# A hybrid decoder trunk on one core: Newton steps, low parts and weight sums on GpSimd, copies and scalings on ScalarE

## The chip, the cores and the metric

The kernel runs on one core of a Trainium2 chip. The core has five engines that work side by side: TensorE (PE, matrix products and transposes; PEld is its weight load), VectorE (DVE), ScalarE (ACT), GpSimd (POOL) and SyncE (SP, which here only issues DMAs). Each engine takes its instructions in order from a queue of its own and waits at an instruction until the semaphores that it needs have been raised. The metric is the device time of one execution in microseconds.

## What is computed

One layer of a decoder for a prompt of 2048 tokens and 8 single sample tokens, with model width 1024, and a final RMSNorm. The reference, cut and shortened to what matters here:

```python
ada = jax.nn.silu(c) @ w_ada + b_ada
shift, scale, gate = jnp.split(ada, 3, axis=-1)
hn = _rmsnorm(x, g_norm) * (1.0 + scale[:, None]) + shift[:, None]
z = hn @ w_in
xa, za, q, k, v, glr, zg = jnp.split(z, SPLITS, axis=-1)
...
xc = conv_b + sum(xp[:, j:j + T] * conv_w[j] for j in range(CONV_W))
gx = sigmoid(blockdiag(xc, w_gate_x) + b_gate_x)
ga = sigmoid(blockdiag(xc, w_gate_a) + b_gate_a)
...
_, h = lax.associative_scan(_lin_comb, (a, u), axis=1)
y_lru = h * jax.nn.silu(za)
...
def step(S, xs):
    qn, kn, vn, dl = xs
    o = jnp.einsum('bhck,bhkv->bhcv', qn, S)
    S = jnp.exp(dl[:, :, 0, :])[..., None] * S + jnp.einsum('bhck,bhcv->bhkv', kn, vn)
    return S, o
...
o = o * lax.rsqrt(jnp.mean(o * o, axis=-1, keepdims=True) + EPS) * g_gla_norm
y_gla = o.reshape(Bn, T, D_GLA) * jax.nn.silu(zg)
mix = jnp.concatenate([y_lru, y_gla], axis=-1) @ w_out
x = x + gate[:, None] * mix
```

There are 4 heads of gated linear attention (GLA; keys 128 wide, values 256) and 8 tiles of 128 channels of the recurrent group (LRU).

## The kernel before

**Halves, heads, chunks.** The prompt is worked in two halves of 1024 tokens. The first has two segments of 512 tokens, the second three of 384, 384 and 264, the last with the 8 samples. In each half the four heads follow each other, in the order 3, 0, 1, 2, with LRU tiles between them. The input projections keep the normalised input on chip as a high and a low part (`hh`, `hl`), split the weights in the same way (`w`), and sum three products for each pair (L327 to L329, L633 to L635). When both halves are done, the output projection runs, as a product of 7 blocks in place of 8 (Strassen and Winograd's scheme) in two halves of the columns; L1452 is its matmul.

**A head's segment.** For each chunk of 128 tokens, `gla_chunk` computes the product of keys and values into the bank `pkv` (L953 to L955) and the output into the bank `po` (L957 to L961), where the last product reads the state `St[h]`. Then VectorE adds `pkv` to the state (L962) and scales it by the chunk's decay (L963), and copies `po` to `on` (L966); ScalarE squares that copy and sums the squares into `ss` (L158). Behind the last chunk of the segment `gla_norm` turns `ss` into an inverse root (`rsqrt`) and scales each chunk of `on` (L974). `gla_out` has PE transpose `on` (L1026), and the result is multiplied by the gate `zs`.

**The inverse root.** `rsqrt` takes a first guess from the bits of the number (L140 to L142) and makes three Newton steps (L144 to L146). The operations are 1 to 4 columns wide and each needs the one before. It is called for the normalisation of x too (`scales`, `times`, where L174 scales x and PE's transposes L188 and L200 read it), 32 times in all.

**Convolution.** `conv` makes the first tap on GpSimd (L1122), three on VectorE (L1124), a high part on ScalarE (`xh`) and a low part on VectorE (`xl`, L1138), for the gates' matmuls (L1150 to L1152).

**Output-weight sums.** `out_weights` multiplies the blocks of `w_out` by the gate `g` and forms the sums of the seven products, in 16 steps: 8 for each half of the columns of a block, the first four of each 8 for the GLA rows, the other four for the LRU rows, where two sums are split into high and low parts as well (L761). A step loads `r` (L735, two loads, one buffer), makes two products of 512 columns and four sums of 256 (L756), and stores the seven results (L769; the split ones at L763). The next load of `r` waits until the stores and sums of the last step are done. `g` is there when the gate has been computed by PE, stored (L700) and loaded again (L716), and a bias has been added (L721).

**What sets the order.** The program is written with a clock of its own: `after(units, f)` puts f off by so many units of projection work, and `tick` runs what has come due. The framework then places the instructions on the engines by what they depend on and by its own idea of durations, so that an instruction may be placed ahead of others that were written earlier. `tc.issue_after(x)` holds an instruction behind x, if both are on the same engine. `behind(q)` gives that for the last instruction written so far on engine q, and `out_weights` uses it:

```python
            with behind(V):
                for f in ops[0]:
                    f()
```

SP's queue carries, in one order, the loads of input weights (`wr`, L285), the stores of split weights (`parts`, L311, each waiting for the split L292 on VectorE), the loads of x, and the loads and stores of `out_weights`.

Of the kernel before, what the change touches and what calls it, by code (L numbers as in the profile page):

```python
# [8 lines left out]
F32 = mybir.dt.float32  # L9
F32R = mybir.dt.float32r  # L10
I32 = mybir.dt.int32
AF = mybir.ActivationFunctionType
OP = mybir.AluOpType
# [36 lines left out]
def hybrid_kernel(ctx, tc, i, o):  # L50
# [84 lines left out]
    def rsqrt(pool, out, ss, n, rows, scale):  # L135

        y = pool.tile([P, 16], F32, tag="rs_y", name="rs_y", bufs=1)[:rows, :n]
        t = pool.tile([P, 16], F32, tag="rs_t", name="rs_t", bufs=1)[:rows, :n]
        x = pool.tile([P, 16], F32, tag="rs_x", name="rs_x", bufs=1)[:rows, :n]
        V.tensor_scalar(x, ss, scale, EPS, op0=OP.mult, op1=OP.add)  # L140
        V.tensor_scalar(t.bitcast(I32), x.bitcast(I32), 1, None, op0=OP.logical_shift_right)
        V.tensor_scalar(y.bitcast(I32), t.bitcast(I32), -1, 0x5F3759DF, op0=OP.mult, op1=OP.add)  # L142
        for it in range(3):
            V.tensor_tensor(t, y, y, op=OP.mult)  # L144
            V.scalar_tensor_tensor(t, t, -0.5, x, op0=OP.mult, op1=OP.mult)
            V.scalar_tensor_tensor(out if it == 2 else y, t, 1.5, y, op0=OP.add, op1=OP.mult)  # L146


    gls = hnp.tile([P, TH + NS], F32R, name="gls")
# [559 lines left out]
    def out_weights():  # L709
# [39 lines left out]
        def step(s, r, g):  # L749
            t = hp.tile([P, 3, 256], F32, tag="t", name="t")  # L750
            b11, b12, b21, b22 = r[:, 0, 0], r[:, 0, 1], r[:, 1, 0], r[:, 1, 1]
            q, f, m = where(s)
            c = slice(q * 256, q * 256 + 256)

            def op(*a):
                return lambda: V.tensor_tensor(*a[:3], op=a[3])  # L756

            def split(n, x):
                p = hp.tile([P, 2, 256], F32R, tag="p", name="p", bufs=2)
                S.copy(p[:, 0], x)  # L760
                V.tensor_tensor(p[:, 1], x, p[:, 0].bitcast(F32), op=OP.subtract)  # L761
                for h in range(2):
                    SP.dma_start(wd2[n, :, h, m, c], p[:, h].bitcast(F32))  # L763

            def store():
                for x, ops in ((r[:, 0], (B11, T1)), (r[:, 1], (B21, B22)), (t, (T2, T3, T4))):
                    for n, k in enumerate(ops):
                        if not (f and k in (B22, T4)):
                            SP.dma_start(wd[f, k, :, m, c], x[:, n])  # L769
                if s % 8 < 7:  # L770
                    after(1, lambda: again(s + 1, g))
                elif q == 0:
                    after(1, lambda: begin(1))

            one([[op(r[:, 0], r[:, 0], g, OP.mult)], [op(r[:, 1], r[:, 1], g, OP.mult)],
                 [op(t[:, 1], b22, b12, OP.subtract), op(b12, b12, b11, OP.subtract)],
                 [op(t[:, 0], b22, b12, OP.subtract), op(t[:, 2], b21, t[:, 0], OP.subtract)]]
                + ([[lambda: split(0, b22)], [lambda: split(1, t[:, 2])]] if f else []), store)
# [165 lines left out]
    def gla_chunk(half, h, s, c, prep, run, v):  # L944

        qi, _, f, _ = prep
        kT, on, ss = run
        first = half == 0 and s == 0 and c == 0
        t = slice(c * P, (c + 1) * P)
        pkv = psum.tile([P, 512], F32, tag="kv", name="pkv", bufs=1)[:, :DV]  # L950
        tt = SEGS[half][s][0] // P + c
        vh, vl = [x[tt // 4][:, tt % 4] for x in v]
        PE.matmul(pkv, kT[0][:, t], vh, start=True, stop=False)  # L953
        PE.matmul(pkv, kT[0][:, t], vl, start=False, stop=False)
        PE.matmul(pkv, kT[1][:, t], vh, start=False, stop=True)  # L955
        po = psum.tile([P, 512], F32, tag="o", name="po", bufs=1)[:, :DV]
        PE.matmul(po, amh[:, c], vh, start=True, stop=False)  # L957
        PE.matmul(po, amh[:, c], vl, start=False, stop=False)
        PE.matmul(po, aml[:, c], vh, start=False, stop=first)
        if not first:  # L960
            PE.matmul(po, qi[:, t], St[h], start=False, stop=True)  # L961
            V.tensor_tensor(St[h], St[h], pkv, op=OP.add)  # L962
            V.tensor_scalar(St[h], St[h], f[:, c + 1:c + 2], None, op0=OP.mult)  # L963
        else:
            V.tensor_scalar(St[h], pkv, f[:, c + 1:c + 2], None, op0=OP.mult)
        V.tensor_copy(on[:, c], po)  # L966
        square_sum(xp, ss[:, c:c + 1], on[:, c], P, DV)

    def gla_norm(nch, run):
        _, on, ss = run  # L970
        rs = gp.tile([P, 4], F32, tag="ors", name="ors")
        rsqrt(gp, rs[:, :nch], ss[:, :nch], nch, P, 1.0 / DV)
        for c in range(nch):
            V.tensor_scalar(on[:, c], on[:, c], rs[:, c:c + 1], None, op0=OP.mult)  # L974

    def sample_state(h, smp, b0, st, done):

# [129 lines left out]
    def lru_units(half, last_a=None):  # L1107
# [8 lines left out]
        def conv(j, s, xa, cv, xh, xl):  # L1116
# [18 lines left out]
                        V.scalar_tensor_tensor(cv[:, sm], cs[:, :, k], cw[k], cv[:, sm],  # L1135
                                               op0=OP.mult, op1=OP.add)
            S.copy(xh[:, c], cv[:, c])
            V.tensor_tensor(xl[:, c], cv[:, c], xh[:, c].bitcast(F32), op=OP.subtract)  # L1138

        def gates(t, ss):  # L1140
            j, cv, xh, xl, wgh, wgl, res = t.j, t.cv, t.xh, t.xl, t.wgh, t.wgl, t.res
# [721 lines left out]
```

## Time and profile before

| | |
|---|---|
| median of 3 runs | 1464.42 us (1464.33 to 1464.67) |
| span of the profiled execution | 1461.9 us |
| what lies around the span (median less span) | 2.5 us |
| ACT's copies, casts, squares and other work | 633.1 us busy |
| POOL: all its instructions | 116, of them 40 first taps of the convolution, 47.9 us |
| DVE: L966, 64 copies of `po` | 26.7 us |
| DVE: L962 and L963, 60 each | 24.9 and 20.8 us |
| DVE: L756, 32 of 512 columns | 22.0 us |

The page gives the busy time of each engine and its share of the span; a group's row gives a line of the kernel, the engine, what is written and read, the shape, how often, the busy time in us and the mean ns of one, and behind the last bar how long the engine stood idle just ahead of these instructions and for whom. In a row of the timeline the first number is the start in us from the span's begin, the second the time in us.

### The profile page before, as it was taken

The page shows a single profiled execution, that of the slowest core. Times are in us where ns is not written, and L with a number is a line of the kernel's source. Part 1 is how long each engine was busy: PE and PEld are TensorE (multiplying, and loading weights), DVE is VectorE, ACT ScalarE, POOL GpSimd, SP SyncE. Part 2 cuts the span into 40 slices and gives each one's busy share as a digit, 9 for nine tenths or more (in the row PEclk, how much of TensorE's full clock was granted, in tenths as well). Part 3 has the DMA queues.
Part 4 walks back from the last instruction along what each step waited for, and adds up shares of the span by engine and source line. Part 5 has one row for each costly group of instructions (what it writes and reads, how often), then busy time and mean ns, then how long its engine had stood idle before and what let it go on. Part 6 is the DMA issues. An engine that isn't in the chain of part 4 may idle for free.

```text
span 1461.9 us, 23152 instructions
## 1 busy us (share of the span) xinstructions
PE 1434.5 (98%) x8745; PEld 1270.3 (87%) x8745; DVE 1002.7 (69%) x2390; ACT 633.1 (43%) x1143; POOL 95.3 (7%) x116
## 2 busy tenths in 40 slices
PE   8999999999999999999999999999999999999997
PEld 6888888888898887999999999999998887778886
DVE  5756555764665777667567657576677986688886
ACT  4643532652454366533532542445256522144332
POOL 0200000100100003001001101010011000000000
PEclk9999999999999999999999999999999999999999
DMA  9755554645465554245655545564551767694452
GB/s 324 268 177 173 187 167 145 208 156 166 129 205 189 182 199 140 94 150 172 199 160 173 189 137 174 183 196 139 184 186 63 300 226 275 231 350 143 138 172 101
DMA packets 173606, 268.53 MB, mean 184 GB/s; under 512 B 10483, under 2 KB 126867, under 8 KB 171054
## 3 DMA queue, kind: packets, MB, share of 16 engines
q1 hardware_dynamic: 141093, 250.00, 50.6%
q10 hardware_dynamic: 32048, 16.00, 3.6%
q8 instruction: 69, 1.13, 0.3%
q0 software_dynamic: 352, 1.05, 0.2%
q14 instruction: 44, 0.35, 0.1%
HBM read 168.55 MB, written 98.52 MB: 183 GB/s over the span
## 4 chain that ended last, share of the span: by engine, by line
PE 48%; DVE 5%; ACT 2%; DMA 1%; POOL 1%; issue 0%; ACTq 0%
PE acc L1452 12%; PE tp L1452 9%; PE acc L633 6%; PE acc L635 6%; PE acc L634 6%; PE acc L327 2%; PE acc L328 2%; PE acc L329 2%; DVE cv L1124 1%; PE po L961 1%; DVE tg L1168 1%; POOL cv L1122 1%; PE pss L1658 1%; PE tp L1026 1%; PE acc L1150 0%; PE acc L1151 0%
## 5 line engine op out<-in xcount | busy, mean ns | idle before, releaser
L633 PE MATMUL acc<-hh,w 128*128 128x384 f32 (+2 forms) x1256 | 445.6, 355 | 1.4 <-DVE f L890 1.1
L634 PE MATMUL acc<-hl,w 128*128 128x384 f32 (+2 forms) x1256 | 435.2, 347 | 0.0
L635 PE MATMUL acc<-hh,w 128*128 128x384 f32 (+2 forms) x1256 | 434.2, 346 | 0.0
L633 PEld LDWEIGHTS acc<-hh,w 128*128 128x128 f32 x1256 | 235.9, 188 | 23.3 <-issue 1.6
L635 PEld LDWEIGHTS acc<-hh,w 128*128 128x128 f32 x1256 | 235.9, 188 | 19.6
L634 PEld LDWEIGHTS acc<-hl,w 128*128 128x128 f32 x1256 | 236.0, 188 | 19.3 <-issue 0.4
L1452 PE MATMUL acc<-w,a 128*128 128x512 f32 (+1 forms) x792 | 184.8, 387 | 0.0
L1452 PEld LDWEIGHTS acc<-w,a 128*128 128x128 f32 x792 | 146.8, 188 | 33.2 <-issue 3.4
L327 PE MATMUL acc<-w,hh 128*128 128x256 f32 (+1 forms) x508 | 145.4, 286 | 0.5 <-POOL hh L192 0.4
L329 PE MATMUL acc<-w,hl 128*128 128x256 f32 (+1 forms) x508 | 143.6, 283 | 0.2 <-DVE hl L216 0.2
L328 PE MATMUL acc<-w,hh 128*128 128x256 f32 (+1 forms) x508 | 143.3, 282 | 0.0
L1452 PE MATMUL tp<-w,a 128*128 128x512 f32 x564 | 136.2, 391 | 0.0
L1452 PEld LDWEIGHTS tp<-w,a 128*128 128x128 f32 x564 | 105.2, 188 | 27.1 <-issue 5.2
L1016 ACT ACTIVATE zs<-acc 128x512 f32<-128x512 f32 (+2 forms) x80 | 41.0, 513 | 174.2 <-PE acc L635 168.8
L1124 DVE SCALAR_TENSOR_TENSOR cv<-xa,vecT,cv 128x512 f32<-128x512 f32 (+2 forms) x120 | 77.1, 646 | 41.4 <-POOL cv L1122 41.0
L1017 DVE SCALAR_TENSOR_TENSOR zs<-zs,acc 128x512 f32<-128x512 f32 (+2 forms) x80 | 46.2, 578 | 77.5 <-ACT zs L1016 77.4
L327 PEld LDWEIGHTS acc<-w,hh 128*128 128x128 f32 x508 | 96.0, 189 | 2.5 <-DVE vl L845 0.6
L329 PEld LDWEIGHTS acc<-w,hl 128*128 128x128 f32 x508 | 96.1, 189 | 0.4 <-DVE hl L216 0.4
L328 PEld LDWEIGHTS acc<-w,hh 128*128 128x128 f32 x508 | 95.5, 188 | 0.2
L1122 POOL TENSOR_SCALAR cv<-xa,vecT 128x512 f32<-128x512 f32 (+2 forms) x40 | 47.9, 1197 | 606.1 <-ACT xa L1220 499.8
L1302 ACT CAST a<-s 128x512 fp32r<-128x512 f32 x61 | 36.5, 619 | 96.9 <-issue 32.7
L158 ACT ACTIVATE junk<-on 128x256 bf16<-128x256 f32 x64 | 26.7, 416 | 72.2 <-DVE on L966 63.5
(339 smaller groups left out, 2243.0 us busy)
## 6 DMA issues: line engine op xcount, KB each, us to landing
w<-parts SPq DMA_DIRECT2D x38, 1024.0 KB
parts<-w SPq DMA_DIRECT2D x37, 1024.0 KB
wr<-in_w_in_dram SPq DMA_DIRECT2D x44, 512.0 KB
a<-mixd SPq DMA_DIRECT2D x63, 256.0 KB
w<-wd SPq DMA_DIRECT2D x12, 1024.0 KB
wada<-in_w_ada_dram SPq DMA_DIRECT2D x16, 512.0 KB
r<-in_w_out_dram SPq DMA_DIRECT2D x32, 256.0 KB
mixd<-zs ACTq DMA_DIRECT2D x32, 256.0 KB
```

The lines of the kernel that those rows point to most:

```text
L327: PE.matmul(ps, hh[:, kt, c], hi[:, kt % 4], start=kt == 0, stop=False)
L328: PE.matmul(ps, hh[:, kt, c], lo[:, kt % 4], start=False, stop=False)
L329: PE.matmul(ps, hl[:, kt, c], hi[:, kt % 4], start=False, stop=kt == KT - 1)
L633: PE.matmul(ps[:, :n], hi[:, kt], a, start=kt == 0, stop=False)
L634: PE.matmul(ps[:, :n], hi[:, kt], b, start=False, stop=False)
L635: PE.matmul(ps[:, :n], lo[:, kt], a, start=False, stop=kt == KT - 1)
L1016: S.activation(z, ps, AF.Tanh, scale=0.5)
L1017: V.scalar_tensor_tensor(z, z, 1.0, ps, op0=OP.add, op1=OP.mult)
L1122: G.tensor_scalar(cv[:, cq], xa[:, cq], cw[0], cb, op0=OP.mult, op1=OP.add)
L1124: V.scalar_tensor_tensor(cv[:, cq], xa[:, cq.start + k:cq.stop + k], cw[k], cv[:, cq], op0=OP.mult, op1=OP.add)
L1302: S.copy(t[:, 0, k], (low(t) if src is None else src)[:, k])
L1452: PE.matmul(ps, t[:, u, k], w[:, v, k, c], start=(q < 3 or ps is own) and (k, u, v) == (0, 0, 0), stop=(k, u) == (3, 1), skip_group_check= ...
```

## The change

Five things move. The Newton steps go to GpSimd, as four operations for each of three steps in place of three. The low part `xl` of the convolution goes to GpSimd. So do the products, sums and low parts of `out_weights`. ScalarE scales `pkv` by the decay out of its bank into `kvs` (for all but a head's very first chunk this is the place in `on` that the chunk's output takes next), and VectorE updates the state with one operation, state times decay plus `kvs`. ScalarE copies `po` to `on`, and scales `on` by the inverse root.

```diff
@@ -141,9 +141,10 @@
         V.tensor_scalar(t.bitcast(I32), x.bitcast(I32), 1, None, op0=OP.logical_shift_right)
         V.tensor_scalar(y.bitcast(I32), t.bitcast(I32), -1, 0x5F3759DF, op0=OP.mult, op1=OP.add)
         for it in range(3):
-            V.tensor_tensor(t, y, y, op=OP.mult)
-            V.scalar_tensor_tensor(t, t, -0.5, x, op0=OP.mult, op1=OP.mult)
-            V.scalar_tensor_tensor(out if it == 2 else y, t, 1.5, y, op0=OP.add, op1=OP.mult)
+            G.tensor_tensor(t, y, y, op=OP.mult)
+            G.tensor_tensor(t, t, x, op=OP.mult)
+            G.tensor_scalar(t, t, -0.5, 1.5, op0=OP.mult, op1=OP.add)
+            G.tensor_tensor(out if it == 2 else y, t, y, op=OP.mult)
 
 
     gls = hnp.tile([P, TH + NS], F32R, name="gls")
@@ -753,12 +754,12 @@
             c = slice(q * 256, q * 256 + 256)
 
             def op(*a):
-                return lambda: V.tensor_tensor(*a[:3], op=a[3])
+                return lambda: G.tensor_tensor(*a[:3], op=a[3])
 
             def split(n, x):
                 p = hp.tile([P, 2, 256], F32R, tag="p", name="p", bufs=2)
                 S.copy(p[:, 0], x)
-                V.tensor_tensor(p[:, 1], x, p[:, 0].bitcast(F32), op=OP.subtract)
+                G.tensor_tensor(p[:, 1], x, p[:, 0].bitcast(F32), op=OP.subtract)
                 for h in range(2):
                     SP.dma_start(wd2[n, :, h, m, c], p[:, h].bitcast(F32))
 
@@ -953,17 +954,16 @@
         PE.matmul(pkv, kT[0][:, t], vh, start=True, stop=False)
         PE.matmul(pkv, kT[0][:, t], vl, start=False, stop=False)
         PE.matmul(pkv, kT[1][:, t], vh, start=False, stop=True)
+        kvs = St[h] if first else on[:, c]
+        S.activation(kvs, pkv, AF.Copy, scale=f[:, c + 1:c + 2])
         po = psum.tile([P, 512], F32, tag="o", name="po", bufs=1)[:, :DV]
         PE.matmul(po, amh[:, c], vh, start=True, stop=False)
         PE.matmul(po, amh[:, c], vl, start=False, stop=False)
         PE.matmul(po, aml[:, c], vh, start=False, stop=first)
         if not first:
             PE.matmul(po, qi[:, t], St[h], start=False, stop=True)
-            V.tensor_tensor(St[h], St[h], pkv, op=OP.add)
-            V.tensor_scalar(St[h], St[h], f[:, c + 1:c + 2], None, op0=OP.mult)
-        else:
-            V.tensor_scalar(St[h], pkv, f[:, c + 1:c + 2], None, op0=OP.mult)
-        V.tensor_copy(on[:, c], po)
+            V.scalar_tensor_tensor(St[h], St[h], f[:, c + 1:c + 2], kvs, op0=OP.mult, op1=OP.add)
+        S.copy(on[:, c], po)
         square_sum(xp, ss[:, c:c + 1], on[:, c], P, DV)
 
     def gla_norm(nch, run):
@@ -971,7 +971,7 @@
         rs = gp.tile([P, 4], F32, tag="ors", name="ors")
         rsqrt(gp, rs[:, :nch], ss[:, :nch], nch, P, 1.0 / DV)
         for c in range(nch):
-            V.tensor_scalar(on[:, c], on[:, c], rs[:, c:c + 1], None, op0=OP.mult)
+            S.activation(on[:, c], on[:, c], AF.Copy, scale=rs[:, c:c + 1])
 
     def sample_state(h, smp, b0, st, done):
 
@@ -1135,7 +1135,7 @@
                         V.scalar_tensor_tensor(cv[:, sm], cs[:, :, k], cw[k], cv[:, sm],
                                                op0=OP.mult, op1=OP.add)
             S.copy(xh[:, c], cv[:, c])
-            V.tensor_tensor(xl[:, c], cv[:, c], xh[:, c].bitcast(F32), op=OP.subtract)
+            G.tensor_tensor(xl[:, c], cv[:, c], xh[:, c].bitcast(F32), op=OP.subtract)
 
         def gates(t, ss):
             j, cv, xh, xl, wgh, wgl, res = t.j, t.cv, t.xh, t.xl, t.wgh, t.wgl, t.res
```

Lines between L146 and L956 have a number higher by one in the changed kernel: L757 there is L756 before, L762 is L761, L736 is L735, L770 is L769, L312 and L286 are L311 and L285.

The instructions also take other places on the engines. Three places, each as a row for an instruction (line, operation, what is written and read, shape, how many alike in a row).

First, the Newton steps of the second head's first segment. Before, on VectorE, their end and what follows; `rs_t`, `rs_y` and `ors` are the small tiles of `rsqrt`, `on` is the head's output:

```order
L144 TENSOR_TENSOR rs_t<-rs_y 128x4
L145 SCALAR_TENSOR_TENSOR rs_t<-rs_t,rs_x 128x4
L146 SCALAR_TENSOR_TENSOR ors<-rs_t,rs_y 128x4
L974 TENSOR_SCALAR on<-on,ors 128x256 x4
L1031 SCALAR_TENSOR_TENSOR zs<-tp,gsc,zs 128x512
```

Of the change, on GpSimd, from the end of the Newton steps of the segment before:

```order
L147 TENSOR_TENSOR ors<-rs_t,rs_y 128x4
L757 TENSOR_TENSOR r<-r,g 128x512 x2
L757 TENSOR_TENSOR t<-r 128x256
L757 TENSOR_TENSOR r<-r 128x256
L757 TENSOR_TENSOR t<-r 128x256
L757 TENSOR_TENSOR t<-r,t 128x256
L757 TENSOR_TENSOR r<-r,g 128x512
L144 TENSOR_TENSOR rs_t<-rs_y 128x4
L757 TENSOR_TENSOR r<-r,g 128x512
L145 TENSOR_TENSOR rs_t<-rs_t,rs_x 128x4
L757 TENSOR_TENSOR t<-r 128x256
L146 TENSOR_SCALAR rs_t<-rs_t 128x4
```

The first step of the weight sums now stands ahead of these Newton steps, and the second step's operations stand between them; before, VectorE came to the first step of the sums a whole segment later (the first L756 starts at 273.69 us).

Second, SP's queue behind the load of `g`. Before:

```order
L716 DMA g<-gated 128x2x256
L285 DMA wr<-in_w_in_dram 128x8x128
L245 DMA xt<-in_x_prompt_dram 128x1024
L311 DMA parts<-w 256x1x1024
L285 DMA wr<-in_w_in_dram 128x8x128
```

Of the change; `wd` takes the results of a step:

```order
L717 DMA g<-gated 128x2x256
L286 DMA wr<-in_w_in_dram 128x8x128
L246 DMA xt<-in_x_prompt_dram 128x1024
L770 DMA wd<-r 128x256 x4
L770 DMA wd<-t 128x256 x3
L736 DMA r<-in_w_out_dram 128x2x256 x2
L770 DMA wd<-r 128x256 x4
L770 DMA wd<-t 128x256 x3
L736 DMA r<-in_w_out_dram 128x2x256 x2
L770 DMA wd<-r 128x256 x3
L312 DMA parts<-w 256x1x1024
L286 DMA wr<-in_w_in_dram 128x8x128
```

Two steps' stores and reloads, and part of the third's, now stand between the load of x and the next store and load of weights.

Third, the Newton steps of the same head's second segment. Before, on VectorE, with the low part `xl` of a convolution ahead of them:

```order
L1138 TENSOR_TENSOR xl<-cv,xh 128x512
L140 TENSOR_SCALAR rs_x<-oss 128x4
L141 TENSOR_SCALAR rs_t<-rs_x 128x4
L142 TENSOR_SCALAR rs_y<-rs_t 128x4
L144 TENSOR_TENSOR rs_t<-rs_y 128x4
```

Of the change, on GpSimd:

```order
L1122 TENSOR_SCALAR cv<-xa,vecT 128x512
L757 TENSOR_TENSOR r<-r,g 128x512
L144 TENSOR_TENSOR rs_t<-rs_y 128x4
L145 TENSOR_TENSOR rs_t<-rs_t,rs_x 128x4
L757 TENSOR_TENSOR r<-r,g 128x512
L1138 TENSOR_TENSOR xl<-cv,xh 128x512
L146 TENSOR_SCALAR rs_t<-rs_t 128x4
L757 TENSOR_TENSOR t<-r 128x256
L147 TENSOR_TENSOR rs_y<-rs_t,rs_y 128x4
L762 TENSOR_TENSOR p<-r,p 128x256
```

Another step of the sums (the fifth) now runs between the convolution, its low part and the Newton steps. PE's order in the first half is the same as before.

## The prediction

> **What bounds the kernel now.** I read the page's busy shares first, then the busy time by stretches, then what TensorE waits for.
>
> ```profile
> span 1461.9 us, 23152 instructions
> PE 1434.5 (98%) x8745; PEld 1270.3 (87%) x8745; DVE 1002.7 (69%) x2390; ACT 633.1 (43%) x1143; POOL 95.3 (7%) x116
> ```
>
> TensorE (PE) is busy for all but 27 us of the span. VectorE (DVE) has a third of its time free, GpSimd (POOL) nearly all. The next view gives busy time by stretches; the first number behind the length is PE's.
>
> ```profile
> 0.00:100.00 100.00, 93.31 (x733) 77.23 (x734) 68.11 (x216) 55.09 (x96) 12.87 (x21) 0.97 0.82 277
> 100.00:520.00 420.00, 420.00 (x2332) 361.30 (x2331) 257.84 (x560) 178.37 (x294) 14.64 (x12) 1.00 0.53 170
> 520.00:700.00 180.00, 175.07 (x1225) 161.51 (x1224) 126.36 (x351) 93.95 (x170) 24.00 (x31) 1.00 0.46 153
> 700.00:1080.00 380.00, 375.06 (x2699) 365.32 (x2698) 252.26 (x760) 150.79 (x307) 31.59 (x39) 1.00 0.53 175
> ```
>
> From 100 to 520 us, the first half of the tokens, PE does not pause at all: nothing can be won there, and whatever arrives late there is paid in full. PE pauses 6.7 us at the start and 9.9 us between 520 and 1080. What it waits for on DVE is in the view of waits (total us, times, longest):
>
> ```profile
> PE acc L1151 <- DVE xl L1138: 1.7, 2, 0.9
> PE acc L493 <- DVE am L98: 1.5, 1, 1.5
> PE tp L1026 <- DVE on L974: 1.4, 2, 0.9
> PE acc L633 <- DVE f L890: 1.1, 1, 1.1
> PE po L999 <- DVE on L966: 0.9, 1, 0.9
> PE tp L188 <- DVE xv L174: 0.9, 1, 0.9
> PE tp L200 <- DVE x L174: 0.8, 3, 0.3
> ```
>
> These seven sum to 8.3 us, which is about all that an unburdened DVE can give back. DVE's busy time as such is not on the path. So the question is what the moved work makes late.
>
> **The change part by part.** Prices first. By shape, with the mean ns of one behind the busy time:
>
> ```profile
> L756 DVE TENSOR_TENSOR r<-r,g 128x512 f32<-128x512 f32 x32 | 22.0, 689 | 0.0
> L756 DVE TENSOR_TENSOR t<-r 128x256 f32<-128x256 f32 x32 | 13.4, 419 | 0.3
> L213 POOL TENSOR_SCALAR hh<-hnf 128x512 fp32r<-128x512 f32 x15 | 11.6, 772 | 58.1 <-ACT hnf L209 58.0
> L1848 POOL MEMSET const-float32-0.0<- 128x1 f32 x1 | 0.1, 98 | 0.2 <-issue 0.2
> L974 DVE TENSOR_SCALAR on<-on,ors 128x256 f32<-128x256 f32 x64 | 18.6, 349 | 0.6
> L844 ACT CAST vh<-acc 128x256 fp32r<-128x256 f32 x56 | 20.2, 371 | 82.6 <-PE acc L329 76.7 <-DVE vl L845 3.1 <-DMA mixd<-zs 2.5
> ```
>
> No POOL operation with two tensor inputs stands in the trace. With one input, POOL is near DVE (772 against 689 ns). I bound two inputs by DVE's price and by twice it, and take 1.5 times: 1.03 us for 512 columns, 0.63 for 256. One step of the output-weight sums (two of 512, four of 256) is then 4.6 us, with ends 3.1 and 6.1. [...] A Newton operation on four columns is bounded below by the 98 ns memset and above by 0.3 us; I take 0.25, since each waits for the one before. Twelve are 3.0 us (1.2 to 3.6).
>
> **(a) The start.** Here the Newton steps are on the path: DVE runs them, scales x (L174), and PE waits for the scaled x, twice; then it waits for a DMA.
>
> ```profile
> 9.16 0.16 DVE L144 TENSOR_TENSOR rs_t<-rs_y 128x2 f32<-128x2 f32 x1
> 10.93 1.42 DVE L174 TENSOR_SCALAR x<-x,rs 128x1024 f32<-128x1024 f32 x2
> 12.40 0.55 PE L200 MATMUL tp<-ident,x 128*128 128x128 f32 x3 [0.25 <-DVE x L174]
> 22.93 1.12 PE L200 MATMUL tp<-ident,x 128*128 128x128 f32 x4 [0.31 <-DVE x L174]
> 32.20 1.07 PE L472 MATMUL pa<-wada,sc 128*32 128x128 f32 x30 [0.46 <-DMA wada<-in_w_ada_dram]
> ```
>
> Nine DVE operations take 10.93 - 9.16 = 1.77 us. On POOL: 3.0 and 0.2 for two crossings between engines, so +1.4 each, twice, less the 0.5 that PE then no longer waits for the DMA: **+2.3** (ends -0.6, both waits gone, and +3.6).
>
> **(b) The output-weight sums lose their anchor.** This is the largest term. `behind(V)` ties an instruction to the last VectorE instruction before it, and only if it is on VectorE too. On GpSimd the sums have no tie: the order of the instructions, shown with the change, puts all sixteen steps into the first half, one behind another from the moment `g` exists, with their stores and reloads of `r` in SP's queue, and, in POOL's queue, in front of and between the Newton operations. Where that hurts first is the second head's first segment:
>
> ```profile
> 206.93 0.38 SPq L716 DMA_DIRECT2D g<-gated  x1
> 211.51 0.69 DVE L721 TENSOR_TENSOR g<-g,bt 128x512 f32<-128x512 f32 x1 [1.85 <-DMA g<-gated]
> 219.75 1.14 DVE L974 TENSOR_SCALAR on<-on,ors 128x256 f32<-128x256 f32 x4
> 221.24 1.03 PE L1026 MATMUL tp<-ident,on 128*128 128x128 f32 x8
> 316.57 1.26 SPq L735 DMA_DIRECT2D r<-in_w_out_dram  x2
> ```
>
> PE transposes `on` at 221.24, 1.1 us after its first quarter is scaled (219.75 + 0.35), and PE's own order there is unchanged. In the changed kernel POOL has to do, in this order: step 1 (`g` is there at 212.2, so until 216.8), wait for the reload of `r`, then step 2's six sums with the twelve Newton operations between them. `r` has one buffer, so the reload starts when step 1's last sum is done: 0.4 us for the last store's issue (queued ahead), 0.6 for its own (1.26 for two), and 4.2 to land, as `g` took (207.3 to 211.5). About 5 us: 221.8. Then 4.6 + 3.0 = 7.6: 229.4. ACT's first scaling, 0.4, and PE goes on at 229.8 in place of 221.24: **+8.6**. At the price ends: 212.2 + 3.1 + 5 + 3.1 + 1.2 + 0.4 = 225.0, or 233.4: +3.8 to +12.2.
>
> **(c) The same head's second segment.** The rows of before: the scaling, PE's use, and SP's store of a split weight (L311), which waits for a DVE split.
>
> ```profile
> 251.16 1.14 DVE L974 TENSOR_SCALAR on<-on,ors 128x256 f32<-128x256 f32 x4
> 255.34 1.03 PE L1026 MATMUL tp<-ident,on 128*128 128x128 f32 x8
> 232.33 0.53 SPq L311 DMA_DIRECT2D parts<-w  x1
> ```
>
> Cover was 255.34 - 251.5 = 3.8 us. With everything 8.6 later, step 2 ends near 228, its reload lands at 233, step 3 is done at 237.4. Step 4's load stands behind that L311 in SP's queue (232.33 + 8.6, plus a weight load: 242) and lands at 247; with two convolution splits and a convolution between its sums it ends at 253.5, step 5's `r` lands at 258.8, and step 5, the Newton operations, one `xl` and one split among them (4.6 + 3.0 + 1.0 + 0.6) end at 268.0. PE wants the result at 255.34 + 8.6 = 263.9 and gets it at 268.4: **+4.5** (0.5 to 9). Later steps each stand behind an L311 that moves with PE, so POOL is ahead again by the third head. Weight loads (L285) stand in that queue too. The first that does, and the split (L291, on ACT) that reads its buffer:
>
> ```profile
> 226.54 0.61 SPq L285 DMA_DIRECT2D wr<-in_w_in_dram  x1
> 242.62 1.05 ACT L291 CAST w<-wr 128x1024 fp32r<-128x1024 f32 x1
> ```
>
> Behind step 3's stores it is issued near 237, 2 us later than the shift alone makes it, with a cover of 11 us after 4 of landing. I cost that at nothing, and so ACT's waits for the split sums (`p`): free `acc` banks cover a few us. If that cover is gone, PE waits for weights or banks as long as SP or ACT is held; this belongs to the third rival.
>
> **(d) The other first segments.** One of them:
>
> ```profile
> 348.89 1.14 DVE L974 TENSOR_SCALAR on<-on,ors 128x256 f32<-128x256 f32 x4
> 350.38 1.03 PE L1026 MATMUL tp<-ident,on 128*128 128x128 f32 x8
> ```
>
> Cover 1.1 us. The chain gets longer by 1.2 (Newton), and by some 0.5 because the copy and the scaling are now ACT's, with crossings (371 and 349 ns apiece, so the operations themselves are even): +0.7, three times: **+2.0** (0 to 5). The normalisations at 540 to 580 (`xv`, in the list of waits) cost **+1.5** (0 to 4) likewise.
>
> **(e) What is won.** Work of some 165 us leaves DVE, and ten of sixteen steps leave the second half. Of the 8.3 us that PE waited for DVE, those for `x` and `xv` get worse instead, and `on` now depends on ACT and POOL. From the rest I take **-2.5** (0 to -8). The state update as one operation after ACT's scaled copy is off the path, since two chunks of a head stand 6.6 us apart:
>
> ```profile
> 206.71 0.28 PE L953 MATMUL pkv<-vh,kTh 128*128 128x256 f32 x1
> 213.32 0.28 PE L953 MATMUL pkv<-vh,kTh 128*128 128x256 f32 x1
> ```
>
> The new chain (ACT's copy, DVE's update, each near 0.4) takes about 1 us; had it no such cover, it would cost that on each chunk. The convolutions' `xl` on POOL costs nothing but for its places in (c).
>
> Sum: 2.3 + 8.6 + 4.5 + 2.0 + 1.5 - 2.5 = +16.4 on the profiled span, 1478.3 us. The median of the runs, 1464.4, is 2.5 above the span, so **1481**.
>
> **The rivals.** *Cover holds (not slower):* the reload of `r` lands early enough that the second head's Newton steps end by 220.8. With 212.2, two steps and twelve small operations at the lowest prices (7.4), 1.2 us would remain for it; the decision is at that point, and the 4.2 us of `g` speak against it. Then only (e), at its high end of 8 with 1 lost at the start: 1457. Chance 0.11.
>
> *The losses cancel:* POOL at DVE's price, (b) at 4, the rest near nothing, (e) at 5: 1462 to 1467. Chance 0.09; within 0.2% (2.9 us) is about what a measurement of this kernel can tell from no change.
>
> *Lateness compounds:* POOL slows where DVE runs long two-input operations beside it.
>
> ```profile
> 269.36 2.66 POOL L1122 TENSOR_SCALAR cv<-xa,vecT 128x512 f32<-128x512 f32 x1 [3.25 <-ACT xa L1220]
> 268.61 2.29 DVE L1168 TENSOR_TENSOR_SCAN tg<-xl,tx 128x1024 f32<-128x1024 f32 x1
> ```
>
> A POOL operation of 512 columns takes 2.66 us beside the scan, against 0.77 in L213's mean, so 1.9 more. [...] If the six sums of most steps meet two such delays of 1.9, a step costs 4 us more, all terms sit at their upper ends (3.6 + 12.2 + 9 + 5 + 4 = 34), and ACT's in-order waits for `p` hold up evictions as well: 1498 to 1508. For it: DVE is 61% busy there. Against it: sums have the length of one DVE operation, not of a scan. Chance 0.18.
>
> **How the numbers follow.** The forecast, 1468 to 1496, has 0.62: predicted 1481. Slower by over 0.2% is 0.62 + 0.18 = 0.80, within 0.09, faster 0.11. The range takes in "losses cancel" and the lower part of "compounds": 1463 to 1502.
>
> **What would show it.** PE's waits should name ACT's scaling (`on`, from GpSimd) ahead of the transposes at L1026: one pause of 4 to 12 us near 221 us, one of up to 9 about 35 us later, small ones at 117, 350 and 480, nothing else in the first half. POOL's `r<-r,g` should wait for DMA before each step, and all sixteen steps be over near 420 us. Start: the two waits for `x` at 1.4 us more each. Wrong would be: no pause near 221 (the reload or POOL is faster than I hold), pauses of PE for weights or evictions (SP's or ACT's queue is what hurts), or a second half that wins more than 8 us.

## The result, and the profile after

| | before | after |
|---|---|---|
| median of 4 runs beside each other | 1464.38 us (1463.71 to 1464.67) | 1553.26 us (1552.86 to 1553.85) |
| ratio, 95% interval | | 1.061 (1.0595 to 1.0625) |
| span of the profiled execution | 1461.9 us | 1551.4 us |

The change makes the kernel 6.1% slower. On the spans it is 89.5 us. The first lines of the page of the changed kernel:

```profile
span 1551.4 us, 23293 instructions
PE 1457.9 (94%) x8745; PEld 1281.8 (83%) x8745; DVE 881.4 (57%) x1749; ACT 703.7 (45%) x1335; POOL 331.2 (21%) x664
```

VectorE lost 121 us of work and GpSimd gained 236, and neither is near its limit: GpSimd has 79% of its time free. TensorE runs the same 8745 matmuls. It now stands idle for 93.5 us in place of 27.4 (66.1 more), and it is busy 23.4 us longer with the same work. The two sum to the 89.5.

Where this happens is in the busy time by stretches, cut where the same work stands: PE's transposes L1026 that began at 117.24, 513.61, 651.18 and 1056.22 us begin at 126.99, 592.60, 732.77 and 1141.89. Columns as before: start and end, length, PE's busy time and, behind POOL, the granted clock.

```profile
0.00:110.00 110.00, 95.31 (x740) 79.73 (x741) 59.94 (x167) 56.55 (x100) 26.16 (x81) 0.91 0.76 255
110.00:599.00 489.00, 438.45 (x2325) 369.69 (x2324) 225.97 (x351) 218.06 (x399) 160.63 (x244) 0.94 0.57 185
599.00:782.00 183.00, 173.04 (x1187) 158.66 (x1186) 102.06 (x236) 97.18 (x185) 49.48 (x122) 0.99 0.38 124
782.00:1166.00 384.00, 378.59 (x2724) 367.16 (x2723) 193.06 (x494) 175.48 (x370) 76.87 (x198) 1.00 0.40 135
1166.00:1551.40 385.40, 372.54 (x1777) 306.55 (x1775) 300.37 (x502) 156.45 (x284) 18.06 (x19) 0.99 0.56 195
```

The start takes 10 us more than its 100 of before, the first half 69 more than its 420, and the three stretches behind it 3, 4 and 3.5 more. The first half, in which PE had not paused at all, now has 50.6 us of pauses, and its matmuls take 18.4 us longer. What PE waits for:

```profile
PE tp L1026 <- ACT on L974: 39.0, 8, 13.2
PE tp L201 <- DVE x L175: 5.3, 4, 1.9
PE acc L1151 <- POOL xl L1138: 4.5, 5, 1.4
PE acc L1150 <- ACT xh L1137: 4.4, 2, 4.0
PE pkv L954 <- ACT on L958: 3.2, 2, 2.5
```

How late PE begins the transposes L1026 in the first half, place by place (starts in us):

| head, segment | before | after | later by |
|---|---|---|---|
| first, 1 | 117.24 | 126.99 | 9.8 |
| first, 2 | 154.59 | 168.25 | 13.7 |
| second, 1 | 221.24 | 244.85 | 23.6 |
| second, 2 | 255.34 | 288.83 | 33.5 |
| third, 1 | 350.38 | 412.60 | 62.2 |
| third, 2 | 384.48 | 457.64 | 73.2 |
| fourth, 1 | 479.51 | 557.64 | 78.1 |
| fourth, 2 | 513.61 | 592.60 | 79.0 |

The first line of the waits is the place that the prediction named: ACT's scaling of `on`, for which the inverse root comes from GpSimd. The timeline at the second head's first segment, on GpSimd, ScalarE and PE:

```profile
236.45 1.26 POOL L757 TENSOR_TENSOR r<-r,g 128x512 f32<-128x512 f32 x1 [4.78 <-DMA r<-in_w_out_dram]
237.67 0.20 POOL L144 TENSOR_TENSOR rs_t<-rs_y 128x4 f32<-128x4 f32 x1
...
244.06 0.20 POOL L147 TENSOR_TENSOR ors<-rs_t,rs_y 128x4 f32<-128x4 f32 x1
244.29 1.70 ACT L974 ACTIVATE on<-on,ors 128x256 f32<-128x256 f32 x4 [11.98 <-POOL ors L147]
244.85 2.52 PE L1026 MATMUL tp<-ident,on 128*128 128x128 f32 x8 [9.33 <-ACT on L974]
```

Read it from below: PE waits 9.33 us for ACT, ACT 11.98 for GpSimd, and GpSimd had stood 4.78 us at a product of the weight sums, for the reload of `r`, with the Newton operations queued behind it and one after each sum. The eight transposes then take 2.52 us in place of 1.03. The view of busy time by stretches of 5 us shows why:

```profile
245.00:250.00 5.00, 5.00 (x18) 4.07 (x19) 3.44 (x5) 2.88 (x6) 3.61 (x3) 0.50 0.62 196
250.00:255.00 5.00, 5.00 (x20) 4.05 (x20) 0.78 (x1) 0.88 (x3) 2.77 (x4) 0.87 0.86 277
```

Behind the pause the granted clock is 0.50 until about 251 us: PE works for 6.4 us at half speed and so pays, as an estimate, another 3.2. How long must a pause be for that? These traces give no single length. The two rows are of the changed kernel. Behind the first, a pause of 3.16 us, eight transposes take 1.16 us, near the 1.03 of full speed, and the granted clock stays at 1.00. Behind the second, a pause of only 1.18 us, it is 0.50 from 128.4 to 131.8 us.

```profile
365.66 1.16 PE L928 MATMUL tp<-xb,e 128*128 128x128 f32 x8 [3.16 <-DVE xb L913]
126.99 2.36 PE L1026 MATMUL tp<-ident,on 128*128 128x128 f32 x8 [1.18 <-ACT on L974]
```

So the length of one pause doesn't settle it: the clock is 1.00 behind 3.16 us and 0.50 behind 1.18. The granted clock behind the pause has to be read.

The third head, where the prediction had GpSimd ahead again, is the worst place. The timeline of SP's queue, GpSimd, VectorE, ScalarE and PE:

```profile
391.55 0.99 SPq L312 DMA_DIRECT2D parts<-w  x1
392.59 0.61 SPq L286 DMA_DIRECT2D wr<-in_w_in_dram  x1
393.55 0.93 SPq L770 DMA_DIRECT2D wd<-r  x1
394.59 2.09 SPq L770 DMA_DIRECT2D wd<-t  x3
394.59 0.17 DVE L142 TENSOR_SCALAR rs_y<-rs_t 128x4 int32<-128x4 int32 x1
399.73 1.26 SPq L736 DMA_DIRECT2D r<-in_w_out_dram  x2
403.07 2.48 POOL L757 TENSOR_TENSOR r<-r,g 128x512 f32<-128x512 f32 x2 [10.82 <-DMA r<-in_w_out_dram]
...
411.80 0.20 POOL L147 TENSOR_TENSOR ors<-rs_t,rs_y 128x4 f32<-128x4 f32 x1
412.04 1.71 ACT L974 ACTIVATE on<-on,ors 128x256 f32<-128x256 f32 x4 [16.90 <-POOL ors L147]
412.60 2.52 PE L1026 MATMUL tp<-ident,on 128*128 128x128 f32 x8 [13.23 <-ACT on L974]
```

A store and a load of input weights stand in SP's queue between the stores of one step, so the last of them goes out late, the reload is issued at 399.73, and GpSimd stands 10.82 us where it had stood 4.78. The head's Newton operations could have begun near 395: VectorE makes their first guess at 394.59.

### The profile page after: what moved, and what is told of

Same layout as the page of the kernel before. It is cut to its first block, busy times and chain, and to the rows that moved or that the text cites. A ratio compares the mean times of both kernels' runs of the same rounds, so it can differ in the third digit from the quotient of the medians.

```text
span 1551.4 us, 23293 instructions
## 1 busy us (share of the span) xinstructions
PE 1457.9 (94%) x8745; PEld 1281.8 (83%) x8745; DVE 881.4 (57%) x1749; ACT 703.7 (45%) x1335; POOL 331.2 (21%) x664
## 4 chain that ended last, share of the span: by engine, by line
PE 45%; DVE 3%; POOL 2%; ACT 2%; issue 1%; DMA 1%; SPq 0%; ACTq 0%; POOLq 0%; DVEq 0%
PE acc L1452 11%; PE tp L1452 8%; PE acc L634 5%; PE acc L636 5%; PE acc L635 5%; PE acc L328 1%; PE acc L329 1%; PE acc L330 1%; DVE cv L1124 1%; PE po L964 1%; POOL cv L1122 1%; DMA a<-mixd 1%; PE pss L1658 1%; PE tp L928 0%; POOL xl L1138 0%
## 5 line engine op out<-in xcount | busy, mean ns | idle before, releaser
L1124 DVE SCALAR_TENSOR_TENSOR cv<-xa,vecT,cv 128x512 f32<-128x512 f32 (+2 forms) x120 | 84.2, 705 | 44.8 <-POOL cv L1122 44.1
L757 POOL TENSOR_TENSOR r<-r,g 128x512 f32<-128x512 f32 x32 | 46.1, 1458 | 147.4 <-DVE g L722 74.0
L974 ACT ACTIVATE on<-on,ors 128x256 f32<-128x256 f32 x64 | 27.8, 498 | 108.9 <-POOL ors L147 108.9
```

What stands on the lines that cost most here:

```text
L757: return lambda: G.tensor_tensor(*a[:3], op=a[3])
L1124: V.scalar_tensor_tensor(cv[:, cq], xa[:, cq.start + k:cq.stop + k], cw[k], cv[:, cq], op0=OP.mult, op1=OP.add)
```

## The experiments

Each kernel is the one before with the edit shown, unless it says the change. Two readings stood against each other at first. By the one, called theory A, nearly all of the loss is the lost tie of the weight sums: their order, and the reloads of `r` ahead of the heads' Newton steps. By the other it is what runs on GpSimd, wherever it is placed. The four kernels with fills leave the products and sums of the output projection's weights out; all others compute everything.

### The parts alone

**All but the sums.** The change with the weight sums on VectorE again, tied as before:

```diff
-                return lambda: G.tensor_tensor(*a[:3], op=a[3])
+                return lambda: V.tensor_tensor(*a[:3], op=a[3])
...
-                G.tensor_tensor(p[:, 1], x, p[:, 0].bitcast(F32), op=OP.subtract)
+                V.tensor_tensor(p[:, 1], x, p[:, 0].bitcast(F32), op=OP.subtract)
```

> All of the change, but the output-weight sums and their low parts stay on VectorE, tied as before. Theory A (the sums, untied, run early and stand ahead of Newton steps and convolutions on GpSimd; they make most of the 89 us): the first half loses only what the Newton steps and ScalarE's part cost by themselves, 1480 to 1498 us, no pause of PE over 4 us at L1026. Theory B (the price of small operations and crossings on GpSimd makes most of it, wherever the sums stand): over 1515 us, pauses of 5 us and more at L1026 stay.

Measured: 1509.36 us, 1.031 (1.0287 to 1.0334), +44.7. It lies between the two. The sums make half of the loss, 1553.3 - 1509.4 = 44 us, and about as much stays without them, where the prediction had +5.8 for (a), (d) and the turn, and -2.5 for (e).

**The sums alone.** The reverse edit, made to the kernel before (`behind(V)` stays in the text, and ties nothing that is on GpSimd).

> Only the sums and their low parts go to GpSimd; Newton steps, xl and the copies stay where they were. Theory A in its narrow form (Newton steps wait behind the sums on GpSimd): with the Newton steps on VectorE nothing of that is left, so at most 1480 us, from convolutions behind sums. Theory A in a wide form (SP's queue and ScalarE's waits for p hurt as well): 1485 to 1515 us, with pauses of PE for xh, xa, w or acc in the first half. Theory B: about 1464 us, since no small operation is moved.

Measured, in one run: 1510.08 us, +45.5. PE's two longest pauses are 11.32 and 9.83 us. GpSimd, VectorE and PE around the first:

```profile
248.27 2.53 POOL L756 TENSOR_TENSOR r<-r,g 128x512 f32<-128x512 f32 x2 [9.87 <-DMA r<-in_w_out_dram]
253.24 0.77 POOL L1122 TENSOR_SCALAR cv<-xa,vecT 128x512 f32<-128x512 f32 x1
254.05 1.21 DVE L1124 SCALAR_TENSOR_TENSOR cv<-xa,vecT,cv 128x512 f32<-128x512 f32 x1 [10.89 <-POOL cv L1122]
265.65 1.61 DVE L974 TENSOR_SCALAR on<-on,ors 128x256 f32<-128x256 f32 x4
266.15 0.45 PE L1026 MATMUL tp<-ident,on 128*128 128x128 f32 x1 [11.32 <-DVE on L974]
```

Here the Newton steps are on VectorE, and the head is late all the same: a convolution's first tap (L1122) stands on GpSimd behind a product that waits 9.87 us for `r`; VectorE's next tap waits 10.89 for it, with state updates, copies and the head's Newton steps queued behind. The in-order queue passes the wait from GpSimd to VectorE to PE, where it is 11.32 us.

**The Newton steps alone.**

```diff
-            V.tensor_tensor(t, y, y, op=OP.mult)
-            V.scalar_tensor_tensor(t, t, -0.5, x, op0=OP.mult, op1=OP.mult)
-            V.scalar_tensor_tensor(out if it == 2 else y, t, 1.5, y, op0=OP.add, op1=OP.mult)
+            G.tensor_tensor(t, y, y, op=OP.mult)
+            G.tensor_tensor(t, t, x, op=OP.mult)
+            G.tensor_scalar(t, t, -0.5, 1.5, op0=OP.mult, op1=OP.add)
+            G.tensor_tensor(out if it == 2 else y, t, y, op=OP.mult)
```

> Only the Newton steps go to GpSimd. Theory A: the start loses what it lost in the changed kernel, 8 to 9 us, each first segment of the first half 1 to 3, the turn between the halves 3 to 6: 1476 to 1488 us. Theory B: over 1500 us.

Measured: 1491.87 us, 1.0186 (1.0171 to 1.0201), +27.2. The start shows the mechanism; VectorE first, then PE's pauses:

```profile
12.20 1.42 DVE L175 TENSOR_SCALAR x<-x,rs 128x1024 f32<-128x1024 f32 x2 [3.38 <-POOL rs L147]
```

```profile
13.09 1.47 PE L201 MATMUL tp<-ident,x 128*128 128x128 f32 x4 [1.91 <-DVE x L175]
26.71 1.47 PE L201 MATMUL tp<-ident,x 128*128 128x128 f32 x4 [1.95 <-DVE x L175]
57.01 0.30 PE L201 MATMUL tp<-ident,xt 128*128 128x128 f32 x1 [1.30 <-DVE xt L175]
67.99 0.30 PE L201 MATMUL tp<-ident,x 128*128 128x128 f32 x1 [1.42 <-DVE x L175]
```

VectorE waits 3.38 us for the root on GpSimd, where its own nine operations took 1.77: 1.6 more for each normalisation. PE feels that at four places, 6.6 us together, where before it waited under 1. From 22 to 32 us the matmuls are slow as well. The stretch, first before and then here; the granted clock is 0.93 and 0.50:

```profile
22.00:32.00 10.00, 8.58 (x109) 6.04 (x101) 6.87 (x16) 4.06 (x6) 1.89 (x3) 0.93 1.03 319
```

```profile
22.00:32.00 10.00, 7.93 (x82) 6.03 (x82) 3.28 (x7) 2.60 (x4) 2.97 (x13) 0.50 1.04 317
```

The first transposes of a head come 11.2 us later than before (128.48 in place of 117.24).

**ScalarE's part alone**: `kvs`, the one-operation update, the copy of `po` and the scaling of `on` (the third and fourth pieces of the change's diff).

> Only ScalarE's part: scaled copy of pkv, copy of po, scaling of on, and the state update as one VectorE operation. Both theories: within 5 us of before, 1460 to 1469 us; if ScalarE's in-order queue is a cost by itself, 1470 us or more, with pauses of PE for on at L1026 or for pkv and po.

Measured: 1467.13 us, 1.0016 (1.0007 to 1.0026). Its page:

```profile
PE 1437.1 (98%) x8745; PEld 1270.2 (87%) x8745; DVE 956.5 (65%) x2198; ACT 706.6 (48%) x1335; POOL 94.1 (6%) x116
```

VectorE has 46 us less to do than before, and nothing is won.

**The low part `xl` alone.**

```diff
-            V.tensor_tensor(xl[:, c], cv[:, c], xh[:, c].bitcast(F32), op=OP.subtract)
+            G.tensor_tensor(xl[:, c], cv[:, c], xh[:, c].bitcast(F32), op=OP.subtract)
```

> Only the convolution's low parts go to GpSimd. If the parts add up, the 45 us of all but the sums are 27 (Newton) + 2.5 (ScalarE) + 15 for this part: 1475 to 1482 us, with pauses at L1150 and L1151. If it costs nothing by itself and the parts hurt together instead, 1464 to 1468 us.

Measured: 1471.43 us, 1.0045 (1.003 to 1.0061), +7.0.

So the four parts alone cost 27.2 + 45.5 + 2.5 + 7.0 = 82 us, and together 89: they nearly add. The loss is not one accident of order but four prices.

**Of the Newton steps, those of the heads alone** (`rsqrt` gets the engine as an argument; the normalisations of x and of the samples stay on VectorE).

> Newton steps on GpSimd for the heads' outputs alone; the normalisation of x and of the samples keeps them on VectorE. Theory: of the 27 us the start (11) and the turn of the halves (4) go, so 1464.5 + 10 to 13 = 1474 to 1478 us, the rest lost in the second half. Rival (each call costs alike, 24 of 32 stay): 1483 us or more.

Measured: 1471.95 us, 1.0056 (1.0037 to 1.0075), +7.5. The trace before has 33 calls, not 32. The 20 for the segments of heads cost 7.5 of the 27.2, the other 13, for x (9) and the heads' outputs of the samples (4), the remaining 20.

**Of ScalarE's part, the state update alone** (the copy and the scaling stay on VectorE).

> Of ScalarE's part only the scaled copy of pkv and the state update as one operation; the copy of po and the scaling of on stay on VectorE. If the 2.5 us of ScalarE's part come from the scaling and the copy, 1462 to 1465 us; if from the update, 1466 us or more.

Measured: 1469.19 us, 1.0036 (1.0023 to 1.0049). So ScalarE's small loss is the update's, and the copies add none to it. The two intervals touch; whether the copies win a little back isn't settled.

### What the sums cost by

**The tie restored on GpSimd.** The sums alone on GpSimd, but each step behind the last GpSimd instruction written:

```diff
-            with behind(V):
+            with behind(G):
```

> As the run with the sums alone on GpSimd, at the same prices, but tied to the last GpSimd instruction written so far, so that six steps lie in the first half and ten in the second, as before the change. Theory A (the lost tie, not the price): 1462 to 1470 us, no pause of PE over 2 us between 100 and 520 us. Rival (price of sums on GpSimd, or its convolutions behind them, wherever they stand): 1490 us or more.

Measured: 1511.27 us, 1.0321 (1.0303 to 1.0338), +46.9. The steps are spread again, six in the first half and ten in the second as before, and nothing is won. Theory A falls: in their old places the sums cost as much. A place in the second half, on GpSimd, VectorE and PE:

```profile
838.29 2.26 POOL L756 TENSOR_TENSOR r<-r,g 128x512 f32<-128x512 f32 x1
```

```profile
837.32 0.62 DVE L1124 SCALAR_TENSOR_TENSOR cv<-xa,vecT,cv 128x384 f32<-128x384 f32 x1
839.32 1.64 DVE L1124 SCALAR_TENSOR_TENSOR cv<-xa,vecT,cv 128x384 f32<-128x384 f32 x1
```

```profile
848.27 0.69 PE L1151 MATMUL acc<-xl,wg 128*128 128x384 f32 x1 [4.39 <-DVE xl L1138]
```

The same VectorE operation takes 0.62 us here beside a first tap on GpSimd (L1122, 1.04 us from 837.28), and 1.64 beside a product on GpSimd, which itself takes 2.26 in place of 1.26. The expectations that follow name this the lock of the two engines, and lay it to GpSimd's reads: a theory, which the kernels with fills test. The taps lie on a chain to PE, and PE pauses 4.39 us behind them. VectorE's busy time gives the size: before, its sums at L756 took 49 us, so without them it should be under 954 us, and it is at 1011. In the runs with fills, below, it is at 961 to 963, so some 50 us of it are longer operations.

**The tie restored in the whole change** (the same edit there).

> All of the change, with that tie. Theory A: about what the change costs without the sums (1509 us), 1505 to 1515; the first segments' pauses at L1026 as short as there. Rival (Newton steps, xl and sums get in each other's way on GpSimd in any order): 1525 us or more.

Measured: 1543.72 us, 1.0542 (1.0506 to 1.0578). The tie gives back about 10 of the 89 us.

**The lost tie by itself**: the kernel before, sums on VectorE, without `with behind(V)`.

> Before, with nothing changed but the tie taken away: the sums stay on VectorE and run early. If the early place costs by itself (reloads of r that an engine waits for, SP's queue), 1480 us or more, with VectorE idle for the DMA of r and pauses of PE in the first half. If it costs only on GpSimd (its price, its lock with VectorE), 1462 to 1470 us.

Measured: 1468.66 us, 1.0027 (1.0016 to 1.0038). The lost tie costs 5 us where the sums run on VectorE.

**Fills in place of the sums.** The tied sums on GpSimd, each operation replaced by two fills of its result, which read nothing:

```diff
-                return lambda: G.tensor_tensor(*a[:3], op=a[3])
+                def two():
+                    for _ in range(2):
+                        G.memset(a[0], 0.0)
+                return two
```

> As the tied sums on GpSimd (1511 us), but each product, sum and low part is replaced by two fills of its result, which read nothing: the output projection's weights are left out. Loads, stores, buffers and places stay. Lock theory (GpSimd's reads and VectorE's two-input operations stretch each other, 64 us on VectorE): VectorE's busy time falls to about 950 us and the time to 1485 us or less. Queue theory (GpSimd waits in order for r, with convolutions behind it, and ScalarE for p): 1500 us or more, with the same pauses.

Measured: 1462.46 us, 0.9992 (0.9983 to 1.0001). The loads, stores and buffers of the sums are all there, VectorE is relieved of 40 us, and the time is that of before: no loss, and no gain.

**ScalarE's wait taken away.** With the tied sums, ScalarE's copy of `p` waits for GpSimd, and PE then for an eviction (`tx`) that is queued behind it. ScalarE and PE there:

```profile
706.79 0.40 ACT L760 CAST p<-r 128x256 fp32r<-128x256 f32 x1 [7.58 <-POOL r L756]
```

```profile
711.12 0.58 PE L327 MATMUL acc<-w,hh 128*128 128x256 f32 x1 [8.97 <-ACT tx L1153]
```

Here that copy is made on GpSimd:

```diff
-                S.copy(p[:, 0], x)
+                G.tensor_scalar(p[:, 0], x, 1.0, 0.0, op0=OP.mult, op1=OP.add)
```

> As the tied sums on GpSimd (1511 us), but the high part p is copied by GpSimd, so that ScalarE waits for no sum. If ScalarE's in-order wait is the loss in the second half (pauses of 9.0 and 1.9 us for tx), 1490 to 1500 us and those two gone; if it is not, 1506 us or more.

Measured: 1514.28 us, 1.0337 (1.032 to 1.0354). PE waits for `tx` no more, and the time is no shorter: ScalarE's wait is not the loss. (The copies are 7.6 us more of GpSimd's work, and read as the sums do.)

**Fills with the sums' waits and length.** The first fills still wait for the reloads of `r` (40.9 us in all, against 32.0 with the sums), since they write into it. But they don't wait for `g`, and they are shorter: GpSimd is busy for 166.2 us in place of 208.8. Here each operation reads one column, so that it waits as the sum did, and two fills follow:

```diff
+                def fill():
+                    one = [x[:, :, :1] if len(x.shape) == 3 else x[:, :1] for x in a[:3]]
+                    G.tensor_tensor(*one, op=a[3])
+                    for _ in range(2):
+                        G.memset(a[0], 0.0)
+                return fill
```

First with the tie (against the tied sums):

> As the tied sums on GpSimd (1511 us), each two-input operation replaced by the same operation on one column and two fills of its result: the same waits and buffers and about the same time on GpSimd, but hardly a read. The output projection's weights are left out. Lock theory: 1460 to 1470 us. Theory that GpSimd's time and order count, and the fills of the last run were only shorter: 1490 us or more.

Measured: 1473.64 us, 1.0069 (1.0043 to 1.0095). GpSimd is as busy as with the sums (210.4 us against 208.8), yet 38 of the 47 us are gone. VectorE's taps of 512 columns, as the groups of the tied sums and of these fills have them (760 ns before; in the kernels with these fills, line numbers in this part are higher by 7):

```profile
L1124 DVE SCALAR_TENSOR_TENSOR cv<-xa,vecT,cv 128x512 f32<-128x512 f32 x48 | 42.7, 890 | 24.0 <-POOL cv L1122 23.9
```

```profile
L1131 DVE SCALAR_TENSOR_TENSOR cv<-xa,vecT,cv 128x512 f32<-128x512 f32 x48 | 36.5, 760 | 24.4 <-POOL cv L1129 24.3
```

So of the tied sums' price, the larger part is GpSimd's reads, not its length or its waits: beside them VectorE's operations last longer (busy time 1011.1 us against 960.6), those with two inputs above all. With the sums and with the fills, the taps of 384 columns take 787 and 617 ns, the products of 512 at L1184 939 and 726; with one input, L963 takes 367 and 350, L974 349 and 353. Beside the fills, where a sum reads one column only, the taps of 512 columns take the 760 of before.

Then without the tie (against the sums alone):

> The same replacement in the run with the sums alone, untied (1510 us). Lock theory alone: 1462 to 1475 us. Queue theory (the convolutions wait behind reloads of r on GpSimd, VectorE behind the convolutions): pauses of PE of 5 to 11 us stay in the first half, 1490 us or more.

Measured: 1489.38 us, 1.0167 (1.015 to 1.0184), +24.9. So of the untied sums' 45.5 us, 25 go with waits, order and length, and 21 with the reads; of the tied sums' 46.9, 9 and 38.

And in the whole change:

> The same replacement in the whole change (1553 us). Lock theory alone: what the change costs without the sums, 1505 to 1515 us. Queue theory (Newton steps and convolutions wait behind reloads of r): the pauses at L1026 of 5 to 13 us stay, 1535 us or more.

Measured: 1524.84 us, 1.0419 (1.0403 to 1.0434), +60.3. Against all but the sums (+44.7) the waits, order and length of the sums cost 15.6 us in the whole change, and the reads another 28.6. PE's pauses at the heads, where L1033 and L981 are L1026 and L974:

```profile
237.27 2.52 PE L1033 MATMUL tp<-ident,on 128*128 128x128 f32 x8 [4.20 <-ACT on L981]
386.85 2.52 PE L1033 MATMUL tp<-ident,on 128*128 128x128 f32 x8 [3.81 <-ACT on L981]
```

At the second head the pause is 4.20 us in place of 9.33, at the third 3.81 in place of 13.23. GpSimd is as busy as with the sums (330.8 us against 331.2), and VectorE is busy 865.2 us against 881.4. How much of the 28.6 comes by these 16 us of longer operations on VectorE, and how much by reloads that come later, isn't separated.

No part and no combination that ran beats the kernel before: among the kernels that compute everything, the best is ScalarE's part alone at 1.0016.

## Why the prediction was wrong, step by step

The direction was right, the forecast of +16.4 us was too small by a factor of five, and 1553 lies far above the range.

**(a) The start, +2.3 forecast, about +10 measured.** The price of a call was nearly right: 1.4 more forecast, 1.6 measured. The 0.2 us in it for two crossings between engines was my estimate, with no row for it; in the run with the Newton steps alone they are 0.12 (0.08 to GpSimd, 0.04 back), and the twelve operations 3.26 where I took 3.0. The count was wrong: I charged two normalisations and took 0.5 off, while PE waits at four, and the clock, which is 0.52 from 12 to 22 us and 0.51 from 22 to 33, was not in the sum.

**(b) The second head's first segment, +8.6 forecast.** Right in mechanism and nearly in size: a pause of 9.33 us, with the reload at 4.78 (5 forecast) and step 2 with the Newton operations at 7.8 (7.6 forecast). Sums on GpSimd cost 1.26 and 0.72 to 0.74 us undisturbed (from 236 to 242 us, while VectorE stands idle), 1.7 to 1.8 times VectorE's 0.69 and 0.42. I took 1.5 times, 1.03 and 0.63, the middle of two bounds of my own: no row of before shows such an operation on GpSimd.

**(c) The second segment, +4.5 forecast.** The pause is 6.34 us, and the lateness grows by 9.9 (23.6 to 33.5), since the half clock behind the pause before is paid as well. The step that failed most is the sentence behind it, that "POOL is ahead again by the third head". From there to the third head the lateness grows by 28.7 us (33.5 to 62.2), with 13.23 of it in the one pause shown, 4.04 and 3.16 in two pauses for a convolution and an input of a head, and most of the rest in shorter pauses and at half clock behind the pauses of 6.34 and 4.04 (0.50 from 288.5 to 292 and from 315 to 319 us); by the head's second segment another 11.0. Later steps do stand behind the stores of split weights in SP's queue, as I said, but that doesn't put GpSimd ahead: the reload comes later, and the Newton operations are queued behind the product that waits for it. PE's lateness was no help to GpSimd, because it also moves the stores that the reload stands behind. The sixteen steps end at 468 us, where about 420 was forecast.

**(d) Other first segments and the turn, +2.0 and +1.5 forecast.** The Newton steps of all heads' segments cost 7.5 us alone; I had charged three segments of the first half only. The turn grows by 2.6 (79.0 to 81.6), within its 0 to 4.

**(e) -2.5 forecast as won.** Nothing was won: 46 us less on VectorE gave 1.0016, 40 us less gave 0.9992, and the stretches behind the first half lost 10.5 us. So an idler VectorE brought back little or nothing of the 8.3 us of waits for it. (The view has four more such waits, of 1.7 us together.)

**What stood with the rivals.** "Lateness compounds" named the right mechanism, VectorE and GpSimd in each other's way, at 0.18. But it priced it by what GpSimd loses, 4 us a step. That gave 1498 to 1508 us, and the time lies above this too. The other side was left out: VectorE's own operations get longer, by some 50 us in the tied kernel, and of these the convolution's taps lie on PE's path. The reads are the largest part of the sums' cost in the tied kernel (38 of 47) and in the whole change (28.6 of 44). The convolution's `xl`, which I costed at nothing but its place, has its own price of 7.0. That PE's clock falls behind pauses stood nowhere in the sum: PE works for 48 us at a granted clock of 0.50 where before it worked for 6, an estimated 21 of the 23.4 us that it is busy longer.

So the failure was one of method too: the sum followed one wait to its end and held the rest of the first half to be covered, though PE had no slack there at all, so that every part had a price. The Newton steps stood at 5.8 in (a), (d) and the turn, and cost 27.2 alone; the sums stood at 13.1 in (b) and (c), and make 44; `xl` stood at nothing.

## What to carry to other kernels

Free time on an engine is no reason to move work there: ask what stands behind the moved work in that engine's queue, above all where an operation waits for a DMA, since every later instruction inherits that wait (here GpSimd's 10.82 us for `r` became 13.23 at PE). The two-input operations that moved from VectorE to GpSimd did not get out of VectorE's way: with the tied sums its taps of 512 columns took 890 ns in place of 760. Replace such operations by fills of the same length and see whether the loss goes; here the taps were at 760 again. And where TensorE never pauses, price each part alone, and look at the granted clock behind each new pause: the time at half speed comes on top of it (6.4 us at 0.50 behind the pause of 9.33).

## What the hardware showed that was not expected

The size of the interference, and on how small operations it falls. In the kernel with the sums alone, GpSimd and VectorE show

```profile
258.43 2.98 POOL L756 TENSOR_TENSOR r<-r,g 128x512 f32<-128x512 f32 x2 [3.71 <-DMA r<-in_w_out_dram]
258.98 1.23 DVE L141 TENSOR_SCALAR rs_t<-rs_x 128x4 int32<-128x4 int32 x1
260.24 1.19 DVE L142 TENSOR_SCALAR rs_y<-rs_t 128x4 int32<-128x4 int32 x1
```

for two operations of four columns with one input, while the one ahead of them in the same chain (L140) takes 0.17 us. They end at 260.21 and 261.43. The two products on GpSimd end at 261.41, and with 1.26 us for the second the first ended, as an estimate, near 260.15. So operations with one input can last longer too, and end about when a product does; under what condition isn't shown. Chained operations of a few columns follow each other on GpSimd every 0.28 us (12 in 3.3 us) where VectorE needs 0.20 (9 in 1.77).
